# A decoder layer in split fp32: the second FFN's first group on the seven-product scheme

## The chip, the cores and the metric

The kernel runs on one NeuronCore of a Trainium2 chip. The metric is the device time of one execution in microseconds (us). The engines are named as in the profile: PE (TensorE), DVE (VectorE), ACT (ScalarE), POOL (GpSimd), SP (SyncE, which issues the DMAs); PEld is PE's weight load, which runs beside its matmuls.

## The reference

The input x is 256 rows of 2048 float32. The layer is a half FFN, a block of three token mixers, an output product and a second half FFN, each added to x:

```python
def swiglu_half_ffn(x, norm_g, w_gate_up, w_down):
    h = rmsnorm(x, norm_g)
    gate, up = jnp.split(h @ w_gate_up, 2, axis=-1)
    return 0.5 * ((jax.nn.silu(gate) * up) @ w_down)
...
        x = x + swiglu_half_ffn(x, ffn1_norm[l], ffn1_w_gate_up[l], ffn1_w_down[l])
...
        x = x + merged @ w_out[l]
        x = x + swiglu_half_ffn(x, ffn2_norm[l], ffn2_w_gate_up[l], ffn2_w_down[l])
```

The FFN's hidden width is 5632, so w_gate_up is 2048 x 11264 and w_down 5632 x 2048; w_out is 2048 x 2048. Everything is float32. The change touches the output product and the beginning of the second FFN.

## The kernel before, in words

**Products.** A float32 factor is cut into a high part (a copy rounded to the type that PE takes, by ACT) and a low part (the difference, by DVE). A product is then three matmuls, high by high, low by high, high by low (`add_product`, L241). The activations, transposed and cut, lie in SBUF as pages of 2 x 128 rows of the inner dimension (`to_lhs_part`, L192: four transposes on PE, a scaled copy on ACT at L189, the difference on DVE at L190, for each half). Weights stream from memory into three `raw` buffers of 1 MB, are cut by ACT (`wh`) and DVE (`wl`) into five buffers each, and PE takes them from there. PE sums in eight PSUM banks; a transpose takes one of them as well.

**Two kinds of group.** `mm_group` (L322) makes 512 output columns from 16 inner blocks: per 512 KB of weights one cut and 12 matmuls. `pair_group` (L248) makes two times 512 columns at once, in eight units of two inner blocks. A plain unit is two cuts of 128 x 1024 and 24 matmuls. A seven-product unit replaces the eight block products of a 2 x 2 scheme by seven: DVE forms sums of the raw weights (ta at L290, tb at L295 and L296), which are cut as well (hah, hal, hbh, hbl), and PE does 21 matmuls, some with the sums of the activation page in place of the page. These are made by `form_page` (L215) from a finished page: seven DVE and ACT steps named fv, ff and form. Units 0, 1 and 2 are of seven products wherever a group has forms. After the last of them four of the eight banks are summed by DVE and ACT (L314 to L318: ua, u3, u4, uv); the other four run to the end of the group. `MIXED = (3, 0, 4, 1, 5, 2, 6, 7)` (L25) is the order of units.

**Side steps.** Small steps (transposes, activation sums) wait in a list, `side`; a group takes one from it at each `tick()` (L75): `mm_group` after each cut, `pair_group` after each plain cut behind the last seven-product unit, or ahead of the first one. `pause` stands for an empty step.

**Order.** The program is written as one stream; the framework's scheduler puts each engine's instructions into a fixed order, and each engine runs its own in that order.

**The place of the change.** The output product (L918 to L932) makes columns 0 to 1023 with two `mm_group`s and columns 1024 to 2047 with one `pair_group`. Each finished 512 columns are added to the residual x (`Stream.added`, L385, the adds at L389), squared and summed by ACT (L364), kept in memory, and handed to `side` as two transposing steps, which make pages x2[0] to x2[7] (`residual`, L392). After the last columns the three activation sums of x2[0], x2[1] and x2[2] go to `side` too (L932). Then `ffn` (L412) runs. Its first 512 hidden columns are made by two `mm_group`s, gate and up (L459 to L463), under which the last four pages are transposed and the activation sums made; groups 1 to 10 are `pair_group`s with the order MIXED (L464). `gated` (L447) makes silu(gate) x up on ACT and DVE. The first FFN runs the same function, with `before`, which loads x between the cuts.

Of the kernel before, what the change touches and what calls it, by code (L numbers as in the profile page):

```python
# [13 lines left out]
ALU = mybir.AluOpType  # L14
# [3 lines left out]
T = 2  # L18
S = 256
D = 2048  # L20
KD = D // P
FF = 5632
NFC = FF // 512
DOWN = (2, 5, 8, 11, 14)
MIXED = (3, 0, 4, 1, 5, 2, 6, 7)  # L25
# [8 lines left out]
def hybrid_layer(  # L34
# [27 lines left out]
    nc = tc.nc  # L62
# [9 lines left out]
    side = deque()  # L72
    pause = [lambda: None]
# [6 lines left out]
    def drain():  # L80
        while side:
            tick()
# [10 lines left out]
    def temp(shape, name, dtype=F32):  # L93
        return tp.tile([P, *shape], dtype, tag="t", name=name)
# [150 lines left out]
                ps, sides[part], wt[i][:, col : col + 512], start=start and q == 0, stop=stop and q == 2  # L245
            )

    def pair_group(w, c0, c1, lhs, forms, order, seven=None, hook=None):  # L248

        seven = list(forms) if seven is None else seven
        at = [i for i, u in enumerate(order) if u in seven]
        acc, terms = {}, {}

        def into(key, last):
            if key not in acc:
                acc[key] = bank("mm")  # L260
                return acc[key], True, last
            return acc[key], False, last

        for i, u in enumerate(order):
            end = i == len(order) - 1
            if hook:
                hook(i, u)
            raw = wp.tile([P, 2, 2, 512], F32, tag="raw", name="raw")
            for n, cc in enumerate((c0, c1)):
                nc.sync.dma_start(  # L270
                    out=raw[:, n, :, :],
                    in_=w[2 * u * P : (2 * u + 2) * P, cc : cc + 512].rearrange("(k p) c -> p k c", p=P),
                )
            if u not in seven:
                for n in range(2):
                    wt = parts(1024)
                    cut(wt, raw[:, n, :, :].rearrange("p k c -> p (k c)"))
                    for t in range(T):
                        for kk in range(2):
                            ps, start, stop = into((t, n), end and kk == 1)  # L280
                            add_product(ps, [lhs(2 * u + kk, q, t) for q in range(2)], wt, kk * 512, start, stop)
                    if not at or i > at[-1] or 1 < i < at[0]:
                        tick()
                continue
            last = i == at[-1]
            s = raw.rearrange("p n k c -> p (n k) c")
            plain = parts(1024)
            cut(plain, s[:, 0:2, :].rearrange("p s c -> p (s c)"))
            ta, tb = page([2, 512], F32, "ta"), page([2, 512], F32, "tb")
            nc.vector.tensor_tensor(ta, s[:, 3:4, :].to_broadcast([P, 2, 512]), s[:, 1:3, :], ALU.add)  # L290
            ha = (page([1024], F32R, "hah"), page([1024], F32R, "hal"))
            cut(ha, ta.rearrange("p s c -> p (s c)"))
            plain2 = parts(512)
            cut(plain2, s[:, 2, :])
            nc.vector.tensor_tensor(tb[:, 0, :], ta[:, 0, :], s[:, 2, :], ALU.add)  # L295
            nc.vector.tensor_tensor(tb[:, 1, :], tb[:, 0, :], s[:, 0, :], ALU.add)  # L296
            hb = (page([1024], F32R, "hbh"), page([1024], F32R, "hbl"))
            cut(hb, tb.rearrange("p s c -> p (s c)"))
            fm = lambda m: [forms[u][:, q, m, :] for q in range(2)]
            xq = lambda kk, t: [lhs(2 * u + kk, q, t) for q in range(2)]  # L300
            for key, sides, wt, col in (
                ("p1", xq(1, 0), plain, 512),
                ((0, 0), xq(0, 0), plain, 0),
                ("p5", fm(0), ha, 0),
                ("p7", fm(2), ha, 512),
                ((0, 1), fm(3), plain2, 0),
                ("p6", fm(1), hb, 0),
                ((1, 0), xq(0, 1), hb, 512),
            ):
                ps, start, stop = into(key, last if isinstance(key, str) else end)  # L310
                add_product(ps, sides, wt, col, start, stop)
            if last:
                a, u3, u4, v = (temp([512], n) for n in ("ua", "u3", "u4", "uv"))
                nc.scalar.activation(a, acc["p1"], AF.Copy)  # L314
                nc.vector.tensor_tensor(u3, acc["p6"], a, ALU.add)
                nc.vector.tensor_tensor(u4, acc["p5"], u3, ALU.subtract)
                nc.vector.tensor_tensor(u3, acc["p7"], u3, ALU.add)
                nc.vector.tensor_tensor(v, acc["p5"], u3, ALU.subtract)  # L318
                terms = {(0, 0): a, (1, 0): u3, (0, 1): u4, (1, 1): v}
        return acc, terms  # L320
# [88 lines left out]
    def form_steps(forms, tiles, n=3):  # L409
        return [lambda j=j: form_page(forms, tiles, j) for j in range(n)]  # L410

    def ffn(lx, forms, rs, wgu, wd, stream, cb, before=None):  # L412
        hid, flat = [], {}
        hdram = dp.tile([NFC - 1, P, 4 * S], F32, tag="hd", name="hd", bufs=2)
        rh = st.tile([P, T], F32, tag="rh", name="rh")
# [31 lines left out]
        def gated(c, gate, up):  # L447
            hd = []
            for t in range(T):
                s = gate[t]  # L450
                if c == 0:
                    s = temp([512], "sg")
                nc.scalar.activation(s, gate[t], AF.Silu, scale=rs[0][:, t : t + 1])
                h = temp([512], "hd") if c == 0 else up[t]
                nc.vector.scalar_tensor_tensor(h, up[t], rh[:, t : t + 1], s, ALU.mult, ALU.mult)
                hd.append(h)
            return hd

        pa = mm_group(wgu, 0, KD, lx, before=before)  # L459
        nc.vector.tensor_scalar(rh, rs[0], 0.5, None, ALU.mult)  # L460
        pb = mm_group(wgu, FF, KD, lx)
        hd = gated(0, [pa[t][0] for t in range(T)], [pb[t][0] for t in range(T)])
        side.extend(put(0, hd))  # L463
        for c in range(1, NFC):  # L464
            if c == NFC - 1:
                side.extend(put_last)
            acc, terms = pair_group(wgu, c * 512, FF + c * 512, lx, forms, MIXED)
            for n in range(2):
                for t in range(T):
                    d = terms[t, n]  # L470
                    nc.vector.tensor_tensor(d, acc[t, n], d, ALU.add)
            hd = gated(c, [terms[t, 0] for t in range(T)], [terms[t, 1] for t in range(T)])
            if c < NFC - 1:
                side.extend(put(c, hd))
            if c == NFC - 2:
                put_last = [lambda: get(0), lambda: get(1)]
# [448 lines left out]
        cb(c, [[ps[t][0]] for t in range(T)])  # L925
    for c in range(2, 4):
        s1.load(c)
    po, terms = pair_group(w_out[0], 1024, 1536, lg, formsg, MIXED)
    side.extend(pause * 2)
    for n in range(2):  # L930
        cb(2 + n, sums(po, terms, n))
    side.extend(form_steps(forms2, x2))  # L932


    def store(c, ps):
# [37 lines left out]
```

## Time and profile before

| What | Value |
|---|---|
| Median of 3 runs | 2131.93 us (2131.91 to 2132.99) |
| The profiled execution: its own time | 2133.13 us |
| its span on the core | 2131.1 us |
| granted TensorE clock, mean | 0.999 |
| PE busy | 2120.6 us, 9710 matmuls |
| DVE busy | 1690.3 us |
| ACT busy | 1172.5 us |
| HBM read | 426.16 MB |

The span runs from the first to the last instruction on the core; the execution's own time is longer by what lies around it. A row of a timeline reads: start in us, length, engine, line, operation, output <- input, shape, and in brackets the idle time just ahead with what ended it. An operation's length overlaps the start of the next on its engine, so what it costs a busy engine is the distance from start to start. In a row of a window, the numbers behind the length are the busy time (and instructions) of PE, PEld, DVE, ACT and POOL, then the granted clock, the DMA share and GB/s.

### The profile page before, as it was taken

What the parts mean: (1) busy time and instruction counts of PE and PEld (TensorE: products, weight loads), DVE (VectorE), ACT (ScalarE), POOL (GpSimd) and SP (SyncE); (2) the same over time, 40 slices, a digit from 0 to 9 for tenths busy, and PEclk for the clock granted to TensorE, in tenths of its full rate; (3) what the DMA queues carried; (4) which work ended last, traced back from release to release, by engine and by line L of the source; (5) the groups of instructions that cost most, each with busy time, mean ns of one, the idle gap of its engine ahead of it and who ended that gap; (6) DMA issues with size and microseconds to landing.
All of it is one profiled execution on the core that took longest, in us unless ns stands there. A gap on an engine that the chain in (4) does not pass through costs nothing.

```text
span 2131.1 us, 26009 instructions
## 1 busy us (share of the span) xinstructions
PE 2120.6 (100%) x9710; PEld 1751.2 (82%) x9710; DVE 1690.3 (79%) x2152; ACT 1172.5 (55%) x1467; POOL 3.5 (0%) x24
## 2 busy tenths in 40 slices
PE   9999999999999999999999999999999999999999
PEld 7888888888888888887788888888888888888887
DVE  7898898889858788667655778687899889989675
ACT  6555555556545565546644555555555555556453
POOL 0000000000000000000000000000000000000000
PEclk9999999999999999999999999999999999999999
DMA  7666666666856654754466656765666666677764
GB/s 262 204 218 212 207 205 220 212 230 219 281 198 219 223 202 145 243 172 148 139 197 197 194 178 213 232 226 199 208 211 206 218 207 217 205 235 245 260 187 154
DMA packets 221122, 444.66 MB, mean 209 GB/s; under 512 B 12270, under 2 KB 13380, under 8 KB 220996
## 3 DMA queue, kind: packets, MB, share of 16 engines
q1 hardware_dynamic: 220704, 442.96, 63.2%
q8 instruction: 76, 1.25, 0.2%
q14 instruction: 50, 0.41, 0.1%
q10 hardware_dynamic: 292, 0.05, 0.0%
HBM read 426.16 MB, written 16.79 MB: 208 GB/s over the span
## 4 chain that ended last, share of the span: by engine, by line
PE 99%; DMA 1%; DVE 1%; ACT 0%; SPq 0%; issue 0%; DVEq 0%; ACTq 0%
PE mm L244 68%; PE mm L352 27%; PE hid L428 1%; DMA raw<-in_ffn_w_gate_up_dram 0%; PE x L200 0%; PE fpt L851 0%; DVE wl L346 0%; PE fav L861 0%; PE mg L200 0%; PE flg L823 0%; PE mav L756 0%; PE mlg L729 0%; PE flg L821 0%; PE fav L863 0%; DVE xr L389 0%; PE fav L862 0%
## 5 line engine op out<-in xcount | busy, mean ns | idle before, releaser
L238 ACT ACTIVATE wh<-raw 128x1024 fp32r<-128x1024 f32 (+1 forms) x560 | 552.9, 989 | 590.9 <-PE mm L244 343.9
L239 DVE TENSOR_TENSOR wl<-raw,wh 128x1024 fp32r<-128x1024 f32 (+1 forms) x560 | 628.7, 1132 | 191.5 <-ACT wh L238 190.4
L244 PE MATMUL mm<-wh,x 128*128 128x512 f32 x2116 | 656.1, 391 | 0.0
L244 PEld LDWEIGHTS mm<-wh,x 128*128 128x128 f32 x2116 | 394.1, 188 | 80.1
L244 PE MATMUL mm<-wl,x 128*128 128x512 f32 x1058 | 410.9, 390 | 0.0
L346 DVE TENSOR_TENSOR wl<-raw,wh 128x1024 fp32r<-128x1024 f32 (+2 forms) x218 | 255.6, 1175 | 160.4 <-ACT wh L345 159.7
L352 PE MATMUL mm<-wh,x 128*128 128x512 f32 (+1 forms) x1216 | 370.5, 383 | 2.3 <-ACT x L189 2.3
L244 PE MATMUL mm<-wh,hid 128*128 128x512 f32 x1168 | 357.5, 390 | 0.0
L345 ACT ACTIVATE wh<-raw 128x1024 fp32r<-128x1024 f32 (+2 forms) x218 | 221.3, 1020 | 239.2 <-PE mm L352 180.0
L352 PEld LDWEIGHTS mm<-wh,x 128*128 128x128 f32 x1216 | 224.0, 188 | 47.7 <-ACT x L189 3.4
L244 PEld LDWEIGHTS mm<-wh,hid 128*128 128x128 f32 x1168 | 218.8, 188 | 45.0
L244 PEld LDWEIGHTS mm<-wl,x 128*128 128x128 f32 x1058 | 198.6, 188 | 41.8
L352 PE MATMUL mm<-wl,x 128*128 128x512 f32 (+1 forms) x608 | 231.0, 381 | 0.2 <-DVE wl L346 0.2
L244 PE MATMUL mm<-wl,hid 128*128 128x512 f32 x584 | 222.4, 389 | 0.0
L352 PEld LDWEIGHTS mm<-wl,x 128*128 128x128 f32 x608 | 114.2, 188 | 21.3 <-DVE wl L346 0.6
L244 PEld LDWEIGHTS mm<-wl,hid 128*128 128x128 f32 x584 | 109.6, 188 | 22.9
L290 DVE TENSOR_TENSOR ta<-raw 128x1024 f32<-128x1024 f32 x92 | 112.1, 1218 | 17.6 <-DMA raw<-in_w_out_dram 6.2
L239 DVE TENSOR_TENSOR hal<-ta,hah 128x1024 fp32r<-128x1024 f32 x92 | 112.2, 1219 | 2.3 <-ACT hah L238 2.3
L238 ACT ACTIVATE hah<-ta 128x1024 fp32r<-128x1024 f32 x92 | 96.9, 1053 | 30.3 <-DVE ta L290 30.2
L239 DVE TENSOR_TENSOR hbl<-tb,hbh 128x1024 fp32r<-128x1024 f32 x92 | 112.1, 1219 | 0.1
L244 PE MATMUL mm<-hah,form 128*128 128x512 f32 x368 | 111.3, 389 | 0.0
L238 ACT ACTIVATE hbh<-tb 128x1024 fp32r<-128x1024 f32 x92 | 96.7, 1051 | 17.7 <-DVE tb L296 17.5
(324 smaller groups left out, 2140.1 us busy)
## 6 DMA issues: line engine op xcount, KB each, us to landing
raw<-in_ffn_w_gate_up_dram SPq DMA_DIRECT2D x322, 512.0 KB, 4.6
raw<-in_ffn_w_down_dram SPq DMA_DIRECT2D x176, 512.0 KB, 4.9
raw<-in_w_in_dram SPq DMA_DIRECT2D x52, 1024.0 KB, 5.0
raw<-in_w_in_dram SPq DMA_DIRECT2D x48, 512.0 KB, 5.1
raw<-in_ffn_w_gate_up_dram SPq DMA_DIRECT2D x14, 1024.0 KB, 5.8
hd<-hf SPq DMA_DIRECT2D x20, 512.0 KB, 5.2
hg<-hd SPq DMA_DIRECT2D x20, 512.0 KB, 8.2
raw<-in_w_mem_kv_dram SPq DMA_DIRECT2D x8, 1024.0 KB, 6.9
```

Of the source, the lines that this page charges most:

```text
L238: nc.scalar.activation(dst[0], src, AF.Copy)
L239: nc.vector.tensor_tensor(dst[1], src, dst[0].bitcast(F32), ALU.subtract)
L244: nc.tensor.matmul(ps, sides[part], wt[i][:, col : col + 512], start=start and q == 0, stop=stop and q == 2)
L290: nc.vector.tensor_tensor(ta, s[:, 3:4, :].to_broadcast([P, 2, 512]), s[:, 1:3, :], ALU.add)
L345: nc.scalar.activation(hv, rv, AF.Copy)
L346: nc.vector.tensor_tensor(lv, rv, hv.bitcast(F32), ALU.subtract)
L352: nc.tensor.matmul(ps[t][i][:, :n], lhs(k, part, t), wt[:, kk, o : o + n], start=k == 0 and q == 0, stop=k == kt - 1 and q == 2,)
L428: nc.tensor.transpose(ps[:, j, t * P : (t + 1) * P], hd[t][:, k * P : (k + 1) * P], ident)
```

## The change

There are three parts. In `ffn`, the two `mm_group`s of the first 512 hidden columns and their gating stay only where `before` is given (the first FFN); the second FFN runs its group 0 as a `pair_group` like the others, with `turned`, which gives out all side steps at once ahead of the second unit. In the output product's `pair_group` the order of units is (0, 3, 1, 4, 2, 5, 6, 7), a side step is taken after every plain cut (`early`), and the activation sums for the second FFN are made by a hook ahead of units 5, 6 and 7. The two pauses ahead of the last transposes are gone.

```diff
-    def pair_group(w, c0, c1, lhs, forms, order, seven=None, hook=None):
+    def pair_group(w, c0, c1, lhs, forms, order, seven=None, hook=None, early=False):
...
-                    if not at or i > at[-1] or 1 < i < at[0]:
+                    if not at or i > at[-1] or 1 < i < at[0] or early:
                         tick()
...
-                if c == 0:
+                if c == 0 and before:
                     s = temp([512], "sg")
...
-        pa = mm_group(wgu, 0, KD, lx, before=before)
-        nc.vector.tensor_scalar(rh, rs[0], 0.5, None, ALU.mult)
-        pb = mm_group(wgu, FF, KD, lx)
-        hd = gated(0, [pa[t][0] for t in range(T)], [pb[t][0] for t in range(T)])
-        side.extend(put(0, hd))
-        for c in range(1, NFC):
+        c1 = 0
+        if before:
+            pa = mm_group(wgu, 0, KD, lx, before=before)
...
+            c1 = 1
+
+        def turned(i, u):
+
+            if i == 1:
+                drain()
+
+        for c in range(c1, NFC):
...
-            acc, terms = pair_group(wgu, c * 512, FF + c * 512, lx, forms, MIXED)
+            acc, terms = pair_group(wgu, c * 512, FF + c * 512, lx, forms, MIXED, hook=None if c else turned)
+            if c == 0:
+                nc.vector.tensor_scalar(rh, rs[0], 0.5, None, ALU.mult)
...
-    po, terms = pair_group(w_out[0], 1024, 1536, lg, formsg, MIXED)
-    side.extend(pause * 2)
+
+    def sums_ahead(i, u):
+        if i in (5, 6, 7):
+            form_page(forms2, x2, i - 5)
+
+    po, terms = pair_group(w_out[0], 1024, 1536, lg, formsg, (0, 3, 1, 4, 2, 5, 6, 7), hook=sums_ahead, early=True)
     for n in range(2):
         cb(2 + n, sums(po, terms, n))
-    side.extend(form_steps(forms2, x2))
```

What this does to the engines' fixed orders is shown at three places. Numbers in names tell buffers of one name apart.

**DVE in the output product's second half.** Before, from the cuts of unit 0 on (raw_11486 is unit 0, raw_11535 unit 4, raw_11570 unit 1):

```order
L239 TENSOR_TENSOR wl_11490<-raw_11486,wh_11489 128x1024
L239 TENSOR_TENSOR wl_11501<-raw_11486,wh_11500 128x512
L389 TENSOR_TENSOR xr_11276<-mm_11278,xr_11276 128x512
L290 TENSOR_TENSOR ta_11577<-raw_11570 128x1024
L389 TENSOR_TENSOR xr_11276<-mm_11279,xr_11276 128x512
L239 TENSOR_TENSOR wl_11539<-raw_11535,wh_11538 128x1024
L239 TENSOR_TENSOR hal_11581<-ta_11577,hah_11580 128x1024
L295 TENSOR_TENSOR tb_11578<-ta_11577,raw_11570 128x512
L239 TENSOR_TENSOR wl_11555<-raw_11535,wh_11554 128x1024
L296 TENSOR_TENSOR tb_11578<-tb_11578,raw_11570 128x512
L239 TENSOR_TENSOR wl_11574<-raw_11570,wh_11573 128x1024
L239 TENSOR_TENSOR hbl_11591<-tb_11578,hbh_11590 128x1024
```

Now, from the cuts of unit 1 on (raw_11555 is unit 1, raw_11600 unit 4, raw_11635 unit 2, raw_11699 unit 5, raw_11744 unit 6; line numbers up to 448 are the same before and after):

```order
L295 TENSOR_TENSOR tb_11643<-ta_11642,raw_11635 128x512
L239 TENSOR_TENSOR wl_11865<-raw_11861,wh_11864 128x1024
L389 TENSOR_TENSOR xr_11443<-mm_11475,xr_11443 128x512
L296 TENSOR_TENSOR tb_11643<-tb_11643,raw_11635 128x512
L389 TENSOR_TENSOR xr_11445<-mm_11487,xr_11445 128x512
L389 TENSOR_TENSOR xr_11445<-mm_11538,xr_11445 128x512
L389 TENSOR_TENSOR xr_11443<-ua_11680,xr_11443 128x512
L239 TENSOR_TENSOR wl_11883<-raw_11861,wh_11882 128x1024
L239 TENSOR_TENSOR hbl_11656<-tb_11643,hbh_11655 128x1024
L239 TENSOR_TENSOR wl_11944<-raw_11940,wh_11943 128x1024
L239 TENSOR_TENSOR wl_11955<-raw_11940,wh_11954 128x512
L315 TENSOR_TENSOR u3_11681<-mm_11491,ua_11680 128x512
```

The sums ta and tb of a seven-product unit stood ahead of its plain cuts; now those of unit 1 stand behind the cuts of units 4, 2 and 5 (tb behind unit 6's first one too). raw_11600, raw_11699 and raw_11744 are the same one of the three raw buffers, one after the other, and unit 7 follows in it.

**DVE at the boundary of the output product and the second FFN.** Before, from the adds of columns 1024 to 1535 on (xr_11443 and xr_11445 are the residual's last two blocks of columns, wl rows at L346 the second FFN's first cuts):

```order
L389 TENSOR_TENSOR xr_11443<-mm_11454,xr_11443 128x512
L389 TENSOR_TENSOR xr_11443<-mm_11461,xr_11443 128x512
L190 SCALAR_TENSOR_TENSOR x2_11749<-x2_11750,cols_108,x2_11749 128x256
L389 TENSOR_TENSOR xr_11443<-ua_11695,xr_11443 128x512
L389 TENSOR_TENSOR xr_11443<-u3_11696,xr_11443 128x512
L346 TENSOR_TENSOR wl_11896<-raw_11867,wh_11895 128x1024
L389 TENSOR_TENSOR xr_11445<-mm_11472,xr_11445 128x512
L389 TENSOR_TENSOR xr_11445<-mm_11479,xr_11445 128x512
L346 TENSOR_TENSOR wl_11924<-raw_11921,wh_11923 128x1024
L389 TENSOR_TENSOR xr_11445<-u4_11697,xr_11445 128x512
L389 TENSOR_TENSOR xr_11445<-uv_11698,xr_11445 128x512
L346 TENSOR_TENSOR wl_11950<-raw_11921,wh_11949 128x1024
```

Now, from the second FFN's cut of unit 4 on (mm_11495 is the last bank of the output product to be finished, x2_11298 a finished page):

```order
L290 TENSOR_TENSOR ta_11947<-raw_11940 128x1024
L227 TENSOR_TENSOR form_11696<-ff_11690,form_11696 128x512
L368 TENSOR_REDUCE x2r_11842<-x2ss_11081 128x2
L227 TENSOR_TENSOR form_11741<-ff_11735,form_11741 128x512
L170 TENSOR_SCALAR x2v_11844<-x2r_11842 128x2
L227 TENSOR_TENSOR form_11786<-ff_11780,form_11786 128x512
L174 TENSOR_SCALAR x2a_11847<-x2v_11844 128x2
L190 SCALAR_TENSOR_TENSOR x2_11900<-x2_11901,cols_108,x2_11900 128x256
L190 SCALAR_TENSOR_TENSOR x2_11910<-x2_11911,cols_108,x2_11910 128x256
L175 TENSOR_SCALAR x2y_11846<-x2a_11847 128x2
L190 SCALAR_TENSOR_TENSOR x2_11920<-x2_11921,cols_108,x2_11920 128x256
L190 SCALAR_TENSOR_TENSOR x2_11930<-x2_11931,cols_108,x2_11930 128x256
```

And further on, behind ten 128-wide and other form steps, ta_11947 and the three L227, up to the split of page x2_11900 (the first of the four pages made from xr_11443 and xr_11445):

```order
L239 TENSOR_TENSOR wl_12108<-raw_12104,wh_12107 128x1024
L179 SCALAR_TENSOR_TENSOR x2y_11846<-x2a_11847,x2y_11846 128x2
L239 TENSOR_TENSOR hal_12035<-ta_12031,hah_12034 128x1024
L295 TENSOR_TENSOR tb_12032<-ta_12031,raw_12024 128x512
L239 TENSOR_TENSOR wl_12119<-raw_12104,wh_12118 128x512
L177 TENSOR_TENSOR x2a_11847<-x2y_11846 128x2
L296 TENSOR_TENSOR tb_12032<-tb_12032,raw_12024 128x512
L178 SCALAR_TENSOR_TENSOR x2a_11847<-x2a_11847,x2v_11844 128x2
L179 SCALAR_TENSOR_TENSOR x2y_11846<-x2a_11847,x2y_11846 128x2
L239 TENSOR_TENSOR wl_12162<-raw_12158,wh_12161 128x1024
L478 TENSOR_SCALAR rh_11860<-x2y_11846 128x2
```

The adds stood one behind the other among the second FFN's first cuts; now the adds of xr_11443 wait for mm_11495, and the activation sums, ta_11947 and hal_11951 stand between these adds and the last split of x2_11900.

**PE at the same boundary.** Before, around the transposes of xr_11443 and xr_11445 (mm_11831 and mm_11832 are gate sums of the second FFN's first group):

```order
L352 MATMUL mm_11832<-wh_11895,x2_11749 128x512 x2
L352 MATMUL mm_11832<-wl_11896,x2_11749 128x512
L352 MATMUL mm_11832<-wh_11895,x2_11749 128x512
L200 MATMUL x2_11912<-ident_89,xr_11443 128x128 x4
L200 MATMUL x2_11940<-ident_89,xr_11445 128x128 x4
L200 MATMUL x2_11966<-ident_89,xr_11445 128x128 x4
L352 MATMUL mm_11831<-wh_11923,x2_11885 128x512
L352 MATMUL mm_11831<-wl_11924,x2_11885 128x512
L352 MATMUL mm_11832<-wh_11923,x2_11885 128x512
L352 MATMUL mm_11832<-wl_11924,x2_11885 128x512
```

Now, from the last matmuls of the output product on (mm_11868 belongs to the second FFN):

```order
L244 MATMUL mm_11495<-wh_11792,mg_11129 128x512 x2
L244 MATMUL mm_11495<-wl_11793,mg_11129 128x512
L244 MATMUL mm_11868<-wl_11944,x2_11298 128x512
L200 MATMUL x2_11901<-ident_89,xr_11443 128x128
L200 MATMUL x2_11911<-ident_89,xr_11443 128x128
L200 MATMUL x2_11921<-ident_89,xr_11445 128x128
L200 MATMUL x2_11931<-ident_89,xr_11445 128x128
L200 MATMUL x2_11921<-ident_89,xr_11445 128x128 x3
L200 MATMUL x2_11931<-ident_89,xr_11445 128x128 x3
L200 MATMUL x2_11901<-ident_89,xr_11443 128x128 x3
L200 MATMUL x2_11911<-ident_89,xr_11443 128x128 x3
L244 MATMUL mm_11886<-wh_11954,form_11696 128x512 x2
```

Before, plain products of pages that were ready stood ahead of and between the transposes; now all 16 follow upon the last products of mm_11495 and one of mm_11868, and the products behind them take form_11696 and x2_11900.

More of the change, by code (lines that the diff above doesn't have):

```diff
@@ L450, in gated @@
                 s = gate[t]
-                if c == 0:
+                if c == 0 and before:
                     s = temp([512], "sg")
                 nc.scalar.activation(s, gate[t], AF.Silu, scale=rs[0][:, t : t + 1])
-                h = temp([512], "hd") if c == 0 else up[t]
+                h = temp([512], "hd") if c == 0 and before else up[t]
                 nc.vector.scalar_tensor_tensor(h, up[t], rh[:, t : t + 1], s, ALU.mult, ALU.mult)
@@ L457, in gated @@
             return hd
-        pa = mm_group(wgu, 0, KD, lx, before=before)
-        nc.vector.tensor_scalar(rh, rs[0], 0.5, None, ALU.mult)
-        pb = mm_group(wgu, FF, KD, lx)
-        hd = gated(0, [pa[t][0] for t in range(T)], [pb[t][0] for t in range(T)])
-        side.extend(put(0, hd))
-        for c in range(1, NFC):
+        c1 = 0
+        if before:
+            pa = mm_group(wgu, 0, KD, lx, before=before)
+            nc.vector.tensor_scalar(rh, rs[0], 0.5, None, ALU.mult)
+            pb = mm_group(wgu, FF, KD, lx)
+            hd = gated(0, [pa[t][0] for t in range(T)], [pb[t][0] for t in range(T)])
+            side.extend(put(0, hd))
+            c1 = 1
[3 more added lines that the diff above has]
+        for c in range(c1, NFC):
             if c == NFC - 1:
                 side.extend(put_last)
-            acc, terms = pair_group(wgu, c * 512, FF + c * 512, lx, forms, MIXED)
+            acc, terms = pair_group(wgu, c * 512, FF + c * 512, lx, forms, MIXED, hook=None if c else turned)
+            if c == 0:
+                nc.vector.tensor_scalar(rh, rs[0], 0.5, None, ALU.mult)
             for n in range(2):
```

## The prediction

> **What bounds the kernel now.** The page's busy line and its chain come first.
>
> ```profile
> PE 2120.6 (100%) x9710; PEld 1751.2 (82%) x9710; DVE 1690.3 (79%) x2152; ACT 1172.5 (55%) x1467; POOL 3.5 (0%) x24
> PE 99%; DMA 1%; DVE 1%; ACT 0%; SPq 0%; issue 0%; DVEq 0%; ACTq 0%
> ```
>
> TensorE (PE) is the whole chain, so a matmul less is time saved, and any wait of PE is time lost that nothing gives back. The waits by engine, for PE over the whole span, show how few there are; all five lie outside the stretch that changes.
>
> ```profile
> PE mm L352 <- ACT x L189: 2.3, 2, 1.2
> PE qT L582 <- DVE uv L318: 1.5, 1, 1.5
> ...
> PE mm L352 <- DVE wl L346: 0.2, 1, 0.2
> ```
>
> The busy time by stage, for the output product's second half, the second FFN's first group and its second group (columns: us, PE, weight loads, VectorE (DVE), ScalarE (ACT), POOL, clock, DMA):
>
> ```profile
> 1380.50:1435.00 54.50, 54.50 (x250) 45.13 (x249) 46.11 (x64) 30.29 (x43) 0.00 (x0) 1.00 0.70 237
> 1435.00:1468.50 33.50, 33.50 (x153) 27.84 (x152) 26.12 (x45) 20.58 (x27) 0.00 (x0) 1.00 0.58 189
> 1468.50:1510.80 42.30, 42.30 (x192) 34.99 (x191) 35.42 (x39) 24.04 (x27) 0.00 (x0) 1.00 0.63 211
> ```
>
> PE is busy throughout; DVE has 8.4 + 7.4 = 15.8 us free in the first two stages. The pace of PE comes from the chain in order of time (start, length, matmuls):
>
> ```profile
> 1505.50 38.82 PE mm L244 x171
> 1544.32 0.44 PE hid L428 x4
> ```
>
> A 512-wide matmul takes 38.82 / 171 = 0.227 us, a 128-wide transpose 0.44 / 4 = 0.11 us. The pace of DVE comes from the timeline where it runs without a gap; there start to start counts, not the length.
>
> ```profile
> 1373.26 1.22 DVE L239 TENSOR_TENSOR hal<-ta,hah 128x1024 fp32r<-128x1024 f32 x1
> 1374.40 0.68 DVE L295 TENSOR_TENSOR tb<-ta,raw 128x512 f32<-128x512 f32 x1
> 1375.00 1.22 DVE L239 TENSOR_TENSOR wl<-raw,wh 128x1024 fp32r<-128x1024 f32 x1
> ...
> 1410.65 0.69 DVE L315 TENSOR_TENSOR u<-mm,ua 128x512 f32<-128x512 f32 x1 [0.51 <-PE mm L244]
> ...
> 1412.39 0.69 DVE L316 TENSOR_TENSOR u<-mm,u 128x512 f32<-128x512 f32 x1
> 1413.11 0.69 DVE L317 TENSOR_TENSOR u<-mm,u 128x512 f32<-128x512 f32 x1
> ...
> 1432.28 0.29 DVE L221 TENSOR_TENSOR ff<-fv 128x128 f32<-128x128 f32 x1
> 1432.48 0.29 DVE L223 TENSOR_TENSOR ff<-fv 128x128 f32<-128x128 f32 x1
> ...
> 1437.69 0.15 DVE L178 SCALAR_TENSOR_TENSOR x2a<-x2a,x2v 128x2 f32<-128x2 f32 x1
> 1437.76 1.26 DVE L190 SCALAR_TENSOR_TENSOR x<-x,cols,x 128x256 fp32r<-128x256 f32 x3
> 1438.94 0.68 DVE L227 TENSOR_TENSOR form<-ff,form 128x512 fp32r<-128x512 f32 x1
> ```
>
> So 1024-wide operations cost 1.14 us (1373.26 to 1374.40), 512-wide ones 0.60 (1374.40 to 1375.00), a step of the product sums that needs the one before 0.72, 128-wide ones 0.20, a split of half an activation page (L190) 1.18 / 3 = 0.39, a two-column one 0.07.
>
> **The change: matmuls and engine load.** Three units of the first group go from 24 matmuls to 21: 9 x 0.227 = 2.0 us off PE. The order counts 9 fewer, and the transposes are the same 16. DVE gets 23 instructions more: per unit four 1024-wide and three 512-wide instead of two 1024-wide, 3 x (4 x 1.14 + 3 x 0.60 - 2.28) = 12.2 us, and once four sums at 0.72 and four adds at 0.60, 5.3 us: 17.5 us against the 15.8 us free in the two stages that hold them. ACT gets seven instructions, under 1.1 us each, into a stage where it is busy 20.58 of 33.50 us, and SP eight issues more for the same bytes; both cost nothing as long as DVE is what ends later. Moving the three activation sums (L215) changes where in the queue they stand, not their number.
>
> **The change: DVE's queue at the boundary.** DVE and PE take their queues in order, and front.md's rows show what stands there now. PE ends the output product with matmuls into mm_11495, goes to the 16 transposes, and then to products with x2_11900, made from those. On DVE the add of mm_11495 (L389) stands first, and behind it everything until the second L190 of x2_11900. That L190 frees the bank for PE's matmuls into mm_11964 (from the last matmul into mm_11491, which releases L315, 52 PE instructions stand ahead of the first of them). DVE's work between L315 and that L190, in its order: L315 and L316 0.72 each, L317, L389, L318 and L219 0.60 each, two 1024-wide cuts 1.14 each, 6.1 us; then ten 512-wide (6.0), three 1024-wide (3.4), twelve 128-wide (2.4), five L190 (2.0) and six two-column ones (0.4), 14.2 us. L315 begins 0.43 us after the matmul that it waits for:
>
> ```profile
> 1410.22 0.39 PE L244 MATMUL mm<-hbl,form 128*128 128x512 f32 x1
> ```
>
> The chain is 0.4 + 6.1 + 14.2 = 20.7 us, to which I add 0.1 for the last end. PE has 36 matmuls and 16 transposes for that time, 36 x 0.227 + 16 x 0.11 = 9.9 us. The difference, 10.9 us, is PE waiting. Lower end: if DVE were exactly on time at the add of mm_11495, 0.4 + 14.2 against 17 matmuls and 16 transposes (5.6 us), 9 us. Upper end: ACT's four row sums and three form copies stand between the adds and the L190s too; if they trail by two of them, 13 us.
>
> **The change: the loads.** There are three raw buffers. Now units 1 and 2 are cut plainly at once but summed (ta, tb) only after the cuts of three other units, so each holds its buffer until then, and units 4, 5, 6 and 7 follow each other through one buffer. A pair of loads lands 5.3 us after its issue, and two cuts on ACT take 2.0 us:
>
> ```profile
> 1377.98 0.88 SPq L270 DMA_DIRECT2D raw<-in_w_out_dram  x2
> ...
> 1383.28 1.23 DVE L290 TENSOR_TENSOR ta<-raw 128x1024 f32<-128x1024 f32 x1 [1.78 <-DMA raw<-in_w_out_dram]
> ...
> 1386.12 1.99 ACT L238 ACTIVATE wh<-raw 128x1024 fp32r<-128x1024 f32 x2
> ```
>
> One turn of that buffer is 5.3 + 2.0 + 1.2 (DVE's part of the second cut) = 8.5 us, two turns from unit 5 to unit 7 17.0 us. PE has 58 instructions from the first product of unit 5 to that of unit 7, four of them transposes: 12.7 us. Of the 4.3 us missing, unit 5's lead takes some, and the sums that DVE does between its two cuts of unit 6 (1.14 + 0.60) add some. I take 3.5, between 0 (a full lead) and 7 (no lead, and unit 7's load shares the DMA queues).
>
> **The change: the clock after a wait.** The one place where PE now stands half idle is followed by a lower granted clock (windows of 2 us; the clock is the number after POOL):
>
> ```profile
> 806.00:808.00 2.00, 1.50 (x15) 1.27 (x13) 2.00 (x3) 2.00 (x4) 0.00 (x0) 1.00 0.16 58
> 808.00:810.00 2.00, 0.96 (x8) 0.54 (x6) 2.00 (x4) 2.00 (x8) 0.00 (x0) 1.00 0.86 222
> 810.00:812.00 2.00, 1.51 (x9) 1.27 (x9) 1.97 (x4) 2.00 (x8) 0.00 (x0) 0.74 0.47 184
> 812.00:814.00 2.00, 2.00 (x7) 1.61 (x6) 2.00 (x4) 2.00 (x6) 0.00 (x0) 0.50 0.00 0
> 814.00:816.00 2.00, 2.00 (x9) 1.61 (x9) 2.00 (x6) 2.00 (x5) 0.00 (x0) 0.91 0.03 8
> ```
>
> It cost 2 x (0.26 + 0.50 + 0.09) = 1.7 us. A wait of 10.9 us should bring that once, 1.7 us, between 0 (the clock recovers while PE waits anyway) and twice, 3.4. The Trainium skill (TensorE: Matmul & The Clock Gate, The HAM clock gate) says the same against this change: after an idle window of about 3.4 us the clock is halved, and it takes a busy one to come back; by that rule one return costs an estimated 1.7 us, and the trace agrees. By the rule alone each of the two waits forecast here would pay it, which makes the sum 1.7 us longer.
>
> **The sum.** -2.0 + 10.9 + 3.5 + 1.7 = +14.1 us. The profiled execution took 2133.13 us (span 2131.1, 2.0 outside it), which would become 2147.2; the median of the runs, 2131.93, is 1.2 us lower, so 2146.0. About 0.2% (4.3 us) is what a measurement of this kernel can tell from no change.
>
> **The rivals.** First, only the boundary: unit 5's lead covers the loads and the clock stays up. -2.0 + 10.9 = +8.9, 2140.8. For it: PE's lead over DVE is several buffers deep before 1410 in the rows above (L315 waits for PE there, not PE for DVE). Against: one raw buffer for four units. Chance 0.17. Second, the upper ends together: 13 + 7 + 3.4 - 2.0 = +21.4, 2153.3; for it, that ACT's queue is as full as DVE's there. Chance 0.10. Third, no loss: the 2.0 us come out, 2129.9. This takes that DVE does not hold PE up at the boundary, and it is decided where DVE's work between L315 and the freeing L190 falls under PE's 9.9 us. In the kernel before the same adds, sums and splits lie there and PE never waits, since plain matmuls of the FFN's first half needed only the first pages; now the queue holds PE behind the transposes with 36 matmuls in all. Chance 0.10. More than 4.3 us gained has no term here; 0.03 is for what I do not see. That the change does not do what it says is excluded by the count of matmuls.
>
> **How the numbers follow.** The forecast has 0.60. The range takes the first rival and the lower ends (9 - 2.0 + 0 = +7 and a little less) and stops at the second's time: 2137 to 2153. Slower 0.60 + 0.17 + 0.10 = 0.87; within 0.2% 0.10; faster 0.03.
>
> **What would show it.** In the profile after: PE waits for DVE at the transposes (x L200 <- DVE xr L389) and at the products behind them, with about 11 us of idle PE between the last product of w_out and the first sums of the second FFN; idle on ACT before a cut of raw<-in_w_out_dram, and PE waiting for it; a clock under 1.00 just behind. Wrong would be a PE without waits there (then 2129.9), or waits at other lines, above all in later groups of the FFN, which I take to run as before.

## The result, and the profile after

The changed kernel takes 2146.45 us (median; 2145.3 to 2147.09), beside 2131.91 us for the kernel before on the same chip: a ratio of 1.0064, 95% interval 1.0054 to 1.0075, 14.5 us slower. All times below are medians of the runs at the usual clock; one run of w_mixed took 3049.8 us at a granted clock of 0.65 and is left out. The profiled execution's span is 2145.4 us, 14.3 more than before. The page's busy line and its chain by engine:

```profile
PE 2126.4 (99%) x9701; PEld 1752.5 (82%) x9701; DVE 1706.1 (80%) x2175; ACT 1177.2 (55%) x1474; POOL 3.5 (0%) x24
PE 97%; DVE 1%; DMA 1%; ACT 0%; issue 0%; SPq 0%; ACTq 0%; DVEq 0%
```

Nine matmuls are gone, and yet PE is busy 5.8 us longer: it ran part of them at half speed. PE's share of the chain fell from 99 to 97 per cent; DVE and DMA had 1 per cent each before as well. The largest of PE's waits over the whole span (us, times, longest):

```profile
PE x L200 <- DVE xr L389: 3.4, 2, 2.0
PE mm L352 <- ACT x L189: 2.4, 2, 1.6
PE mm L244 <- ACT wh L238: 1.9, 2, 1.2
PE mm L244 <- DVE form L227: 1.6, 1, 1.6
```

All but the second (which stood in the profile before, far ahead of the change) are new. They form two groups, one at the cuts of late weights (L238), one at the boundary (the adds at L389, the activation sums at L227).

**The first group.** ACT's rows with the wait ahead of them in brackets, then two of the windows of 2 us (us, PE, weight loads, DVE, ACT, POOL, clock, DMA) where PE is short of work:

```profile
1404.19 1.06 ACT L238 ACTIVATE wh<-raw 128x1024 fp32r<-128x1024 f32 x1 [0.93 <-DMA raw<-in_w_out_dram]
...
1413.51 1.06 ACT L238 ACTIVATE wh<-raw 128x1024 fp32r<-128x1024 f32 x1 [2.04 <-DMA raw<-in_w_out_dram]
```

```profile
1404.00:1406.00 2.00, 1.30 (x5) 0.46 (x3) 0.72 (x1) 1.81 (x2) 0.00 (x0) 1.00 0.41 158
...
1414.00:1416.00 2.00, 1.36 (x6) 0.69 (x5) 1.22 (x1) 1.07 (x2) 0.00 (x0) 1.00 1.00 364
```

ACT stands idle until the load of a later unit lands, cuts it, and PE starts right behind. The clock stays at 1.00.

**The second group.** PE from its last product before the transposes, then its windows:

```profile
1433.10 0.40 PE L244 MATMUL mm<-wl,x 128*128 128x512 f32 x1
...
1436.22 0.33 PE L200 MATMUL x<-ident,xr 128*128 128x128 f32 x1 [2.00 <-DVE xr L389]
1437.95 3.15 PE L200 MATMUL x<-ident,xr 128*128 128x128 f32 x12 [1.40 <-DVE xr L389]
1441.63 0.80 PE L244 MATMUL mm<-wh,form 128*128 128x512 f32 x1 [0.52 <-ACT form L226]
1444.05 0.80 PE L244 MATMUL mm<-wh,form 128*128 128x512 f32 x1 [1.62 <-DVE form L227]
...
1448.90 1.90 PE L244 MATMUL mm<-wh,x 128*128 128x512 f32 x5
```

```profile
1434.00:1436.00 2.00, 0.21 (x1) 0.02 (x1) 2.00 (x3) 0.13 (x1) 0.00 (x0) 1.00 0.02 4
1436.00:1438.00 2.00, 0.38 (x2) 0.19 (x2) 2.00 (x4) 0.07 (x1) 0.00 (x0) 0.63 0.59 140
1438.00:1440.00 2.00, 1.93 (x8) 1.53 (x9) 2.00 (x7) 1.11 (x3) 0.00 (x0) 0.50 1.06 413
1440.00:1442.00 2.00, 1.48 (x7) 0.99 (x5) 1.97 (x9) 1.31 (x4) 0.00 (x0) 0.50 1.04 424
1442.00:1444.00 2.00, 0.43 (x1) 0.00 (x0) 2.00 (x5) 2.00 (x7) 0.00 (x0) 0.50 0.18 72
1444.00:1446.00 2.00, 1.96 (x5) 1.57 (x6) 2.00 (x7) 2.00 (x5) 0.00 (x0) 0.50 0.00 0
...
1450.00:1452.00 2.00, 2.00 (x9) 1.66 (x9) 1.81 (x6) 1.16 (x2) 0.00 (x0) 0.96 0.00 0
```

DVE has next to no free time until 1450, while PE waits, transposes, waits again, and then works at half clock. The rows for the queue that the prediction followed: the matmul that releases the first product sum, the cut that DVE was still at, that sum (L315), the cut of the new group's weight sum, which stands in between, and the second split of x2_11900 (the first of the last row's four):

```profile
1428.56 0.39 PE L244 MATMUL mm<-hbl,form 128*128 128x512 f32 x1
...
1428.75 0.69 DVE L239 TENSOR_TENSOR wl<-raw,wh 128x512 fp32r<-128x512 f32 x1 [1.66 <-ACT wh L238]
1429.36 0.68 DVE L315 TENSOR_TENSOR u<-mm,ua 128x512 f32<-128x512 f32 x1
...
1447.03 1.21 DVE L239 TENSOR_TENSOR hal<-ta,hah 128x1024 fp32r<-128x1024 f32 x1
...
1449.44 1.65 DVE L190 SCALAR_TENSOR_TENSOR x<-x,cols,x 128x256 fp32r<-128x256 f32 x4
```

**The size of each term, start to start.** Two marks on PE, the first product of the output product's second half and the first transpose of the third batch of hidden columns, and the kernel's last product, before and after:

```profile
1380.53 0.62 PE L244 MATMUL mm<-wh,mg 128*128 128x512 f32 x2
...
1544.16 0.27 PE L428 MATMUL hid<-ident,u 128*128 128x128 f32 x1
...
2126.15 0.39 PE L244 MATMUL mm<-wl,hid 128*128 128x512 f32 x1
```

```profile
1381.02 0.62 PE L244 MATMUL mm<-wh,mg 128*128 128x512 f32 x2
...
1558.19 0.27 PE L428 MATMUL hid<-ident,u 128*128 128x128 f32 x1
...
2139.96 0.39 PE L244 MATMUL mm<-wl,hid 128*128 128x512 f32 x1
```

The stretch grew from 163.6 to 177.2 us, by 13.5. The rest of the span's 14.3 lies outside: 0.5 had been lost ahead of the first mark, the remainder behind the last product. Within the stretch:

- From 1381.02 to 1433.10 stand 209 matmuls and 8 transposes: 209 x 0.227 + 8 x 0.11 = 48.3 us of work in 52.1, 3.8 us lost at the late loads. (The windows show 2.2 of these as idle; a wait also swallows the overlap that a matmul's length has with the next one's start.)
- mm_11964's first matmul is the 32nd instruction behind 1433.10. In the row of five from 1448.90, at 0.43 us each, it is the fourth: 1450.2. That is 17.1 us for 5.4 us of work, 11.7 us lost at the boundary.
- From there to the second mark the work is 472 x 0.227 + 8 x 0.11 = 108.0 us, and 108.0 us passed: nothing more is lost.
- Of the nine matmuls saved, eight lie in the stretch, 1.8 us. 3.8 + 11.7 - 1.8 = 13.7, beside 13.5 measured.

### The profile page after: what moved, and what is told of

The parts are those of the page before. It is cut to its first block, busy times and chain, and to the rows that moved or that the text cites. A ratio compares the mean times of both kernels' runs of the same rounds, so it can differ in the third digit from the quotient of the medians.

```text
span 2145.4 us, 26046 instructions
## 1 busy us (share of the span) xinstructions
PE 2126.4 (99%) x9701; PEld 1752.5 (82%) x9701; DVE 1706.1 (80%) x2175; ACT 1177.2 (55%) x1474; POOL 3.5 (0%) x24
## 4 chain that ended last, share of the span: by engine, by line
PE 97%; DVE 1%; DMA 1%; ACT 0%; issue 0%; SPq 0%; ACTq 0%; DVEq 0%
PE mm L244 69%; PE mm L352 25%; PE hid L428 1%; DMA raw<-in_ffn_w_gate_up_dram 0%; DMA raw<-in_w_out_dram 0%; DVE wl L239 0%; PE x L200 0%; PE fpt L862 0%; DVE xr L389 0%; DVE wl L346 0%; PE fav L872 0%; ACT wh L238 0%; PE mg L200 0%; PE flg L834 0%; PE mlg L740 0%; PE mav L767 0%
## 5 line engine op out<-in xcount | busy, mean ns | idle before, releaser
L238 ACT ACTIVATE wh<-raw 128x1024 fp32r<-128x1024 f32 x576 | 568.8, 989 | 611.7 <-PE mm L244 367.5
L239 DVE TENSOR_TENSOR wl<-raw,wh 128x1024 fp32r<-128x1024 f32 x576 | 646.4, 1132 | 198.7 <-ACT wh L238 198.2
L244 PE MATMUL mm<-wh,x 128*128 128x512 f32 x2208 | 686.3, 392 | 0.0
L244 PE MATMUL mm<-wl,x 128*128 128x512 f32 x1104 | 427.9, 390 | 0.0
L346 DVE TENSOR_TENSOR wl<-raw,wh 128x1024 fp32r<-128x1024 f32 (+2 forms) x202 | 236.2, 1171 | 153.0 <-ACT wh L345 152.3
L352 PE MATMUL mm<-wh,x 128*128 128x512 f32 (+1 forms) x1088 | 330.5, 382 | 2.4 <-ACT x L189 2.4
L345 ACT ACTIVATE wh<-raw 128x1024 fp32r<-128x1024 f32 (+2 forms) x202 | 204.5, 1017 | 224.2 <-PE mm L352 172.5
L352 PE MATMUL mm<-wl,x 128*128 128x512 f32 (+1 forms) x544 | 206.2, 380 | 0.2 <-DVE wl L346 0.2
L238 ACT ACTIVATE hah<-ta 128x1024 fp32r<-128x1024 f32 x95 | 100.0, 1052 | 23.9 <-DVE ta L290 23.6
L238 ACT ACTIVATE hbh<-tb 128x1024 fp32r<-128x1024 f32 x95 | 99.8, 1051 | 22.3 <-DVE tb L296 22.2
```

The costliest lines, as they stand in the source:

```text
L238: nc.scalar.activation(dst[0], src, AF.Copy)
L239: nc.vector.tensor_tensor(dst[1], src, dst[0].bitcast(F32), ALU.subtract)
L244: nc.tensor.matmul(ps, sides[part], wt[i][:, col : col + 512], start=start and q == 0, stop=stop and q == 2)
L345: nc.scalar.activation(hv, rv, AF.Copy)
L346: nc.vector.tensor_tensor(lv, rv, hv.bitcast(F32), ALU.subtract)
L352: nc.tensor.matmul(ps[t][i][:, :n], lhs(k, part, t), wt[:, kk, o : o + n], start=k == 0 and q == 0, stop=k == kt - 1 and q == 2,)
```

## The experiments

The theory was that of the prediction with these sizes: a queue on DVE that ends at the split of the first late page, and loads that go one after another through one raw buffer. Its rivals: that group 0's three seven-product units are themselves too much for DVE; that the halved clock is a cost of its own; that the side steps, and not the order of units, cause the load wait. Times are given as the difference to the kernel before on the same chip (medians 2132.9, 2132.3 and 2132.2 us in the three sets of runs). Profiled executions are compared from the first mark on, and a loss start to start is counted as above: far ahead of the change, near 810 us, seven of the eleven show 3.4 us at half clock, and no_forms, mixed_early, cuts4 and plain0 show none, 1.7 us that belong to no edit.

**ffn_only: group 0 alone.** The output product as before:

```diff
...
-    po, terms = pair_group(w_out[0], 1024, 1536, lg, formsg, (0, 3, 1, 4, 2, 5, 6, 7), hook=sums_ahead, early=True)
+    po, terms = pair_group(w_out[0], 1024, 1536, lg, formsg, MIXED)
+    side.extend(pause * 2)
...
+    side.extend(form_steps(forms2, x2))
```

> The second FFN's first group as changed (three seven-product units, side steps given out at once), the output product as before the change (order MIXED, no early side steps, activation sums as side steps behind the last transposes). Theory (a queue on DVE at the boundary plus units queued behind one raw buffer, both set by what the output product leaves to DVE): no wait for loads, since the output product's DVE order is the old one. At the boundary DVE has 15.0 us of work (rows of the order at the durations of the prediction) from the first add of the last columns (L389 of mm_11454) to the split that frees the bank for the first new sum, PE has 46 matmuls and 16 transposes, 12.2 us: a wait of about 3.2 us with the 0.4 us of the first start. 2131.9 - 2.0 + 3.2 = 2133.1 us (2130 to 2137). Rival (the seven-product units in group 0 are themselves too much for DVE there, 17.5 us more work than room): the boundary wait stays near 11.5 us, 2131.9 - 2.0 + 11.5 = 2141.4 us.

Measured: 2134.96 us, +2.0 (ratio 1.0009, 1.0001 to 1.0018). The theory's difference was +1.2; the rival's +9.5 is out. PE's waits from 1370 to 1520 are all that is left:

```profile
PE mm L244 <- DVE x L190: 1.8, 2, 1.1
PE mm L244 <- ACT wh L238: 0.6, 1, 0.6
PE mm L244 <- ACT hbh L238: 0.2, 1, 0.2
```

```profile
1420.26 1.45 DVE L389 TENSOR_TENSOR xr<-mm,xr 128x512 f32<-128x512 f32 x2
...
1435.15 0.48 DVE L190 SCALAR_TENSOR_TENSOR x<-x,cols,x 128x256 fp32r<-128x256 f32 x1
1435.55 0.28 DVE L224 TENSOR_TENSOR ff<-ff,fv 128x128 f32<-128x128 f32 x1
```

The wait is at the split that frees the bank, as said, and DVE took 15.3 us to it (1420.26 to 1435.55, the rows of its timeline above; 15.0 expected). Start to start PE lost 2.5 us there (3.2 expected). The two waits for cuts, later in group 0, were not expected: small as they look, PE lost 2.3 us more behind the boundary, and without that the kernel would be close to the one before.

**w_only: the output product's part alone.** Group 0 as before the change:

```diff
...
-        if before:
+        if True:
             pa = mm_group(wgu, 0, KD, lx, before=before)
```

> The output product as changed (new order, early side steps, activation sums ahead), the second FFN's first group as before the change (two mm_groups). Theory: the load wait stays, +3.8 us as measured in the changed kernel (52.1 us from its first product to the last before the transposes, 48.3 us of work). DVE still has the late sums, cuts, activation sums and adds in one queue: 19.2 us from L315 to the first split of page x2[4], against 56 matmuls and 16 transposes (14.5 us) on PE, and a second short wait behind: 5 to 6 us. 2131.9 + 3.8 + 5.7 = 2141.4 us (2138 to 2144). Rival (the boundary wait belongs to the seven-product units of group 0): only the loads, 2135.7 us. Second rival (the output product's part is harmless): 2131.9 us.

Measured: 2142.34 us, +9.4 (ratio 1.0044, 1.0032 to 1.0056); the theory's difference was +9.5. The load wait is the one of the changed kernel (the first row is its longer half), and at the boundary PE waits with two plain mm_groups behind it too (the last line is a window of 10 us there, DVE at 9.90):

```profile
1416.22 1.19 PE L244 MATMUL mm<-wh,mg 128*128 128x512 f32 x4 [1.21 <-ACT wh L238]
1442.31 0.60 PE L352 MATMUL mm<-wl,x 128*128 128x512 f32 x1 [1.69 <-DVE wl L346]
```

```profile
1440.00:1450.00 10.00, 7.44 (x26) 5.12 (x25) 9.90 (x31) 6.71 (x18) 0.00 (x0) 0.83 0.52 180
```

So most of the loss comes from what was done to the output product, not from the seven-product units that the change is named after. The two parts alone make +2.0 and +9.4; together +14.5, 3.1 more than their sum by the medians and 1.4 by the profiled executions (first mark to last product). Why the two together should cost more isn't shown, and it is hardly clear of the noise.

**no_forms: the queue made shorter.** In sums_ahead:

```diff
-            form_page(forms2, x2, i - 5)
+            forms2[i - 5] = formsg[i - 5]
```

> The changed kernel without its three activation sums: the second FFN uses those of the output product's input in their place, so 24 DVE and 3 ACT instructions are left out. Theory: DVE's chain from L315 to the split that frees the bank for mm_11964's successor falls from 20.5 to 14.2 us, the matmuls and the loads stay: 2146.4 - 6.2 = 2140.2 us (2138 to 2142), with the load wait of 3.8 us unchanged. Rival (the halved clock, 13.7 us long here, is a cost of its own and not hidden under DVE's queue): PE at half speed needs at least 6.4 us from the last transpose to that matmul, so only 2.8 us come back, 2143.6 us. Second rival (PE waits for loads and not for DVE): no change, 2146.4 us.

Measured: 2142.10 us, +9.2 (ratio 1.0043, 1.0031 to 1.0055), so by the medians 5.3 us of the 14.5 came back, and the second rival's 0 is out. Between the theory's 6.2 and the rival's 2.8 the medians do not decide, since part of the 5.3 lies elsewhere: from the first mark to the last product the profiled execution is only 3.5 us shorter (755.4 beside 758.9). At the loads it lost 4.5 us start to start, not 3.8; at the boundary 7.4, not 11.7. Those 4.3 us come about in two steps. DVE's chain fell by 4.8 us, from 20.5 to 15.7 (L315 at 1428.64, end of the split at 1444.33); what is missing to 6.2 is ACT, which is now late within the same chain:

```profile
1439.80 0.16 DVE L368 TENSOR_REDUCE x2r<-x2ss 128x2 f32<-128x8 f32 x1 [0.88 <-ACT junk L364]
1440.16 0.88 DVE L190 SCALAR_TENSOR_TENSOR x<-x,cols,x 128x256 fp32r<-128x256 f32 x2 [0.20 <-ACT x L189]
...
1442.20 1.23 DVE L239 TENSOR_TENSOR hal<-ta,hah 128x1024 fp32r<-128x1024 f32 x1 [0.23 <-ACT hah L238]
```

```profile
1430.00:1440.00 10.00, 6.30 (x32) 4.60 (x30) 9.05 (x13) 6.01 (x13) 0.00 (x0) 0.91 0.47 144
1440.00:1450.00 10.00, 9.82 (x33) 7.95 (x34) 9.47 (x23) 6.58 (x12) 0.00 (x0) 0.75 0.42 152
```

DVE waits 1.3 us for the row sums (L364), the splits' first halves (L189) and the high part of the weight sum (hah), which in the changed kernel were ready in time; in the windows it is no longer full. The second step takes back some of the 4.8: PE, still at half speed, comes to the bank an estimated 0.8 us behind the split (the fourth matmul of a row of five that begins at 1444.19), 0.3 in the changed kernel. So the theory has most of it, and where the queue is shorter the halved clock does begin to cost.

**w_mixed: the old order of units.**

```diff
-    ... formsg, (0, 3, 1, 4, 2, 5, 6, 7), hook=sums_ahead, early=True)
+    ... formsg, MIXED, hook=sums_ahead, early=True)
```

> The changed kernel with the old order of units (MIXED) in the output product; early side steps and the sums ahead stay. Theory by order (plain cuts of units 1 and 2 ahead of their sums are what holds the raw buffers): the load wait of 3.8 us goes. Boundary by DVE's rows: 19.0 us from L315 to the freeing split against 43 matmuls and 16 transposes (11.5 us): about 8 us. 2131.9 - 2.0 + 8.0 = 2137.9 us (2136 to 2140). Rival (not the order but the early steps, which take pages from the pool that the weight sums need, make ta and tb late and hold the raw buffers): a load wait of 3 to 4 us stays, 2141.5 us.

Measured: 2139.96 us, +7.0 (ratio 1.0033, 1.002 to 1.0046); +6.0 by the theory, +9.6 by the rival. The windows decide:

```profile
1400.00:1410.00 10.00, 10.00 (x46) 8.29 (x45) 8.67 (x9) 6.83 (x8) 0.00 (x0) 1.00 0.53 185
1410.00:1420.00 10.00, 10.00 (x45) 8.27 (x45) 8.80 (x10) 5.96 (x6) 0.00 (x0) 1.00 0.70 238
1420.00:1430.00 10.00, 10.00 (x46) 8.21 (x44) 9.97 (x15) 4.04 (x6) 0.00 (x0) 1.00 0.75 272
1430.00:1440.00 10.00, 5.21 (x26) 3.54 (x24) 9.97 (x24) 7.27 (x17) 0.00 (x0) 0.85 0.64 210
1440.00:1450.00 10.00, 9.60 (x36) 7.67 (x36) 9.86 (x23) 5.85 (x9) 0.00 (x0) 0.81 0.31 105
```

No wait for loads is left, so it was the order that made it. At the boundary PE lost 8.4 us start to start, beside the 8.0 expected: from L315 to the split DVE needed the 19.0 us of its rows, but it had no free time ahead of them either (9.97 of 10), and L315 began 0.7 us behind its matmul, not 0.4. The new order also made the boundary worse, by 3.3 us (11.7 beside 8.4).

**mixed_early and mixed_sums: the rest of the output product's change, one piece each.** Both have the order MIXED; the first keeps only the side step after every plain cut, the second only the sums ahead (shown against w_mixed):

```diff
 mixed_early
-    ... MIXED, hook=sums_ahead, early=True)
+    ... MIXED, early=True)
...
+    side.extend(form_steps(forms2, x2))
 mixed_sums
-    ... MIXED, hook=sums_ahead, early=True)
+    ... MIXED, hook=sums_ahead)
```

> As ffn_only (group 0 as changed, order MIXED in the output product, activation sums as side steps), and of the output product's change only the side step after every plain cut, without the two pauses. Theory (the queue behind L315): the last matmul into L315's bank moves from the 131st to the 189th of the second half, so the product sums stand in the boundary's queue again; 14.2 us of DVE from L315 to the freeing split against 38 matmuls and 16 transposes (10.4 us): a wait of 4.3 us, up to 5.9 if L315 starts as late as in w_mixed. 2.3 to 3.9 us above the kernel before. Rival (the steps cost nothing, only the activation sums ahead do): as ffn_only, 2.0 us above it.

> As w_mixed, without the side step after every plain cut: order MIXED, activation sums ahead. Theory: L315 is early again (131st), and DVE's queue runs from the first add of the last columns to the freeing split with the activation sums and the first weight sums of the second FFN within it: 18.2 us, against 52 matmuls and 16 transposes (13.6 us): a wait of about 5 us, 3 us above the kernel before (1.5 to 5). Rival (sums made ahead are sums that the boundary need not make): less than ffn_only, under 2.0 us above it.

Measured: mixed_early 2138.34 us, +6.1 (ratio 1.0027, 1.0016 to 1.0037), mixed_sums 2135.46 us, +3.3 (1.0014, 1.0005 to 1.0024). The second is as expected. The first is as to its kind (more than ffn_only, with L315 at 1422.08 and the freeing split 14.2 us behind, as worked out), but 2 us above the range. At the boundary it lost 5.2 us start to start, within the 4.3 to 5.9 expected; another 2.4 us were lost later in group 0, behind a wait of 1.2 us for a cut, as 2.3 were in ffn_only, and the expectation had left these out. In mixed_sums nothing is lost behind the boundary's 4.9 us. So the small piece, transposing two finished pages earlier, costs more than the sums. Why the seven-product units end later with it isn't shown; a possible reason, that the pages taken early are missing for the weight sums, was not tried by itself.

**cuts4 and cuts4_raw4: a raw buffer more.** A fourth raw buffer has room only if the cuts have four buffers instead of five, so that alone is the control:

```diff
 cuts4
-            wp.tile([P, n], F32R, tag="wh", name="wh", bufs=5),
-            wp.tile([P, n], F32R, tag="wl", name="wl", bufs=5),
+            wp.tile([P, n], F32R, tag="wh", name="wh", bufs=4),
+            wp.tile([P, n], F32R, tag="wl", name="wl", bufs=4),
 cuts4_raw4, besides
-            raw = wp.tile([P, 2, 2, 512], F32, tag="raw", name="raw")
+            raw = wp.tile([P, 2, 2, 512], F32, tag="raw", name="raw", bufs=4)
...
-                whole = wp.tile([P, per, ncol], F32, tag="raw", name="raw")
+                whole = wp.tile([P, per, ncol], F32, tag="raw", name="raw", bufs=4)
```

> The changed kernel with four instead of five buffers for each part of a cut, everywhere: the control for the next run, which needs that room. Both theories: the load wait of 3.8 us in the output product stays or grows (3.5 to 6), and the boundary wait of 11.5 us stays. Time 2146 to 2152 us; what matters is the stretch from the first product of the output product's second half to its last.

> The same with four raw buffers instead of three. Theory (units 4 to 7 go one after another through one raw buffer, since units 1 and 2 hold the two others): with a buffer more, PE no longer waits in the output product for a cut of a late load: its idle time there falls from 2 or 3 us to under 0.5, and the time by 3 to 4 us against the run with four cut buffers alone. Rival (DVE's late sums hold PE there, whatever the loads do): the wait stays, under 1 us of difference. The boundary wait stays by both.

Measured: 2147.24 us (2145.0 to 2149.0) and 2141.99 us (2140.9 to 2144.1). In the control the waits for loads are these two:

```profile
1407.26 0.73 PE L244 MATMUL mm<-wh,mg 128*128 128x512 f32 x2 [1.00 <-ACT wh L238]
1408.81 1.20 PE L244 MATMUL mm<-wh,mg 128*128 128x512 f32 x4 [0.35 <-ACT wh L238]
```

With the fourth buffer none is left, and PE is busy in full or within 0.07 us of it in each 10 us from 1380 to 1430. So the missing buffer is the cause of the wait. Its price isn't settled by this pair: start to start the stretch up to the transposes lost 2.3 us in the control, not the 3.5 to 6 expected, and 1.0 with the fourth buffer; the medians differ by 5.2 us, the two profiled executions by 2.5 from the first mark to the last product, and each kernel's own runs scatter by 3 to 4 us.

**plain0: one unit fewer.** ffn_only, with unit 0 of group 0 plain (shown against ffn_only):

```diff
-            ... lx, forms, MIXED, seven=(0, 1, 2), hook=None if c else turned)
+            ... lx, forms, MIXED, seven=(0, 1, 2) if c else (1, 2), hook=None if c else turned)
```

> As ffn_only (output product as before the change), and in the second FFN's first group only units 1 and 2 are of seven products, unit 0 is plain (its first cover of the boundary grows from 45 to 48 matmuls, and the first bank for a new sum is asked for 36 PE instructions later). Theory (PE waits where it asks for the bank that DVE's last splits free): DVE's 15 us from the first add of the last columns are now covered by more than 16 us of matmuls and transposes, so the wait of ffn_only (1.8 us shown, 2.2 from start to start) goes and two thirds of the matmuls' gain stay: 6 x 0.227 = 1.4 us less than the kernel before, 2131.5 us beside its 2132.9 on this chip (2131 to 2133). Rival (DVE has no room for any sums there): 2 us above before or more, 2135 us.

Measured: 2131.03 us beside 2132.26, -1.2 us (ratio 0.9994, 0.9984 to 1.0003). PE has no wait at all from 1370 to 1480, though DVE is as full as before:

```profile
1420.00:1430.00 10.00, 10.00 (x52) 8.40 (x51) 9.47 (x17) 6.50 (x14) 0.00 (x0) 1.00 0.66 230
1430.00:1440.00 10.00, 10.00 (x48) 8.35 (x47) 9.96 (x29) 6.00 (x11) 0.00 (x0) 1.00 0.23 88
```

This is the lowest time of all the kernels here, by about what its six matmuls are worth, and by less than the measurement can tell from no change.

## Why the prediction was right, step by step

| Step | Predicted, us | Measured, us |
|---|---|---|
| nine matmuls less | -2.0 | -2.0 |
| DVE's queue at the boundary | +10.9 (9 to 13) | +11.4 to +11.7 |
| loads through one raw buffer | +3.5 (0 to 7) | +3.8 |
| clock after the wait | +1.7 (0 to 3.4) | 0 to +0.3 |
| sum | +14.1 | +13.5 in the stretch, +14.5 by the medians |

- **The queue.** DVE's time from L315 to the freeing split was 20.3 us by counting (6.1 + 14.2) and 20.5 by the trace (1429.36 to 1449.8). The step held, and ffn_only and w_mixed hit the same sum with other rows (15.3 for 15.0, 19.0 for 19.0). L315 began 0.8 us behind its matmul, not 0.4, since DVE was still at a cut whose high part came late; that is half of the 0.8 us by which the boundary is above the forecast. The transposes and the products behind them were named as the places of the wait, and that is where it was; but the sum puts all of it at the bank, and there PE came 0.3 us after the split. Nor was PE idle for "about 11 us": from 1433.10 to 1450.16 it was idle for 5.8 us and lost the rest at half speed. That PE at half speed and DVE's queue reach the bank within 0.3 us of each other is chance.
- **DVE's load.** The two stages' 17.5 us of work against 15.8 us of room were not the reason by themselves: plain0 keeps DVE at 9.5 to 10 of 10 us (1420 to 1440) with no wait, and ffn_only, with the same work, is 2.0 us slower and not 14.5. What counts is what stands in DVE's queue ahead of the one split that PE asks for, and how many matmuls PE has until it asks.
- **The loads.** ACT idle ahead of cuts of in_w_out_dram and PE right behind it, as foreseen; the cause is borne out twice, by the order (w_mixed) and by the buffer (cuts4_raw4).
- **The clock.** This step failed as a term of the sum. The clock fell as foreseen, and for much longer than the row it was priced from (2 x 2 x (0.37 + 6 x 0.50 + 0.04) = 13.6 us at half speed, instead of 3.4), but it fell during the wait and not behind it. The waits for loads left it at 1.00, so they added no return of their own. From the last wait to the bank PE needed 14 matmuls at 0.43 us, 6.0 us; at full speed it would have waited for DVE's split instead. So nearly all of it was hidden under the queue; no run had this queue at full clock, so this is worked out and not measured. That the sum came out all the same is luck: 0.8 us more at the boundary, 0.3 more at the loads and 0.8 us of span outside the stretch stood in for the 1.7.
- **The first rival**, only the boundary, fell with the load waits. The second, the upper ends together, fell with 11.7 us at the boundary (13) and 3.8 at the loads (7). The third, no loss, fell at its own deciding point: DVE's 20.5 us against PE's 9.9. That the pieces are worth so different amounts, the output product's 9.4 and group 0's 2.0, the prediction did not say; it charged the boundary to the two together.
- Later groups run as before: from the second mark to the last product of the kernel 581.8 us, 582.0 before, the ninth matmul less.

## What to carry to other kernels

Where PE is the whole chain, price a change by the queue of the engine that feeds it: add what stands there, in its fixed order, from the last matmul that it waits for to the instruction that PE waits for, and set it against the matmuls that PE has in between. Moving work earlier in the program is not free: here plain cuts made ahead of their sums cost more than the seven-product units did, in part through the raw buffers that they held, and so did two pages transposed early, for a reason that stays open. And when one part of a change saves matmuls and another rearranges what surrounds it, time them apart: group 0 alone cost 2 us, and with one unit taken back nothing that can be measured.

## What the runs showed of the hardware

In these runs a halved TensorE clock comes in whole pieces of 3.4 us. Twice the time lost in the clock column gives the length at half speed: 3.4 us in w_only (10 x 2 x 0.17), 6.8 in w_mixed (10 x 2 x (0.15 + 0.19)), 6.8 in no_forms (10 x 2 x (0.09 + 0.25)), 13.6 in the changed kernel. There it came back at 1450.16 (2 x 2 x 0.04 us into the last window above), 6.1 us after the last wait ended; counted back from that, its four pieces begin at 1436.52, 1439.93, 1443.34 and 1446.75. The third, with a wait until 1444.05 in it, was followed by another at half speed; the single piece in cuts4, with a wait until 1440.03 in it, was not:

```profile
1443.34:1446.75 3.41, 2.71 (x6) 2.16 (x7) 3.41 (x12) 3.41 (x8) 0.00 (x0) 0.50 0.00 0
...
1439.52:1442.92 3.40, 2.89 (x7) 2.31 (x8) 3.40 (x11) 3.40 (x7) 0.00 (x0) 0.50 0.04 15
```

In these two, 0.7 us without work kept the clock down and 0.5 did not. The piece just ahead of the halving was not idle either: PE was busy in it for 1.23 us in the changed kernel (from 1433.11), and for 1.79 in the kernel before (from 807.55), where no single wait was longer than 1.5 us. The Trainium skill (TensorE: Matmul & The Clock Gate, The HAM clock gate) describes a free-running window of about 3.4 us, of which one busy one ends the throttling; the lengths agree, and these rows show how busy was enough here. The waits for loads, up to 1.2 us each in the changed kernel, left the clock at 1.00.
